# Feed-forward weights that are kept for later, prepared beside the last gates' products instead of beside the branches

## The chip, the cores and the metric

The kernel runs on one core of one Trainium2 chip. The metric is the device time of one execution in microseconds, as the median of several runs. A core has five engines with a queue each: PE (matrix products), DVE (vector), ACT (scalar), POOL (GpSimd) and SP, which here only issues DMA transfers. Every engine takes the instructions of its own queue in order and waits on semaphores for the others.

## The reference

One layer of a decoder trunk on 1040 rows (1024 and 16 meta tokens) of width 1024, in float32. What matters here:

```python
u = rmsnorm(h, mix_norm_pre[l])
proj = u @ w_in[l]
q, f_logit, i_in, g_out, v_pool, gate_a, gate_b = jnp.split(proj, cuts, axis=-1)
a = hgrn2(q, f_logit, i_in, g_out, lbs[l], hgrn_out_norm[l])
p = multiscale_pool(v_pool, pool_proj[l], pool_scale[l])
z = (jax.nn.sigmoid(gate_a) * (a @ w_branch_hgrn[l])
     + jax.nn.sigmoid(gate_b) * (p @ w_branch_pool[l]))
h = h + rmsnorm(z @ w_out[l], mix_norm_post[l])
u = rmsnorm(h, ffn_norm_pre[l])
gt = causal_dwconv(u @ ffn_w_gate[l], ffn_conv_w[l], ffn_conv_b[l])
y = (jax.nn.gelu(gt, approximate=True) * (u @ ffn_w_up[l])) @ ffn_w_down[l]
h = h + rmsnorm(y, ffn_norm_post[l])
```

Every float32 operand of a product is split into two rounded parts (hi and lo, type fp32r), and a product is three matmuls: hi·hi, hi·lo, lo·hi. The split of a weight is a cast on ACT (hi) and a subtraction on DVE (lo).

## The kernel before

The program has these stages in order: norms and the v projection, to about 80 us; the **gates**, to 319.6 us; the **ORDER stage**, to about 552 us; then the product with w_out, the feed-forward part, and the down projection.

*The gates* (class `Strassen`, object `gates`) compute thirteen blocks of `u @ w_in`, named by `GUNITS`: Q0 Q1 G0 A0 A1 A2 F0 F1 A3 B0 B1 B2 B3. Units 8 to 12 are A3, B0, B1, B2, B3. One unit is one level of Strassen's scheme, seven products in the order P1, P2, P6, P5, P3, P7, P4 (24 matmuls of 256 or 258 columns, or 12 of 512), about 19.5 us in all. `product` writes one product into one of four PSUM pairs (`pf`, 4 buffers), then calls `ahead`, which casts and subtracts the weights of the product four places later: names `whi` and `wlo`, three buffers each, two products to a buffer. The raw weights are in `wraw` (three buffers); their Strassen sums `swa`, `swb` are made on GpSimd by `load_unit`, four for a unit. `rest` takes a unit from P6 to P4 and evicts the products on DVE: `p1` += P6; `sg` <- p1, P5 and `sg` += P3 (`put`); `p1` += P7; `sg` <- p1, P5; `sg` <- p1, P4. ACT copies P1 out of PSUM. `between` is a dictionary of functions that `rest` calls after a product; the gates pass none before. In this stage the tile framework's scheduler sets the order of each engine's queue from the program's dependences.

*The ORDER stage* follows a list written by hand: `h0` to `h3` are steps of the four HGRN heads (names `st`, `po`, `al`, `f`, `k`, `q`), `sp` the pooling, PV, G, PP, BB and BA branch products, `sa` the split of a head's output (`ah`, `al`). A `Loader` keeps weight pairs for the products three places ahead: `loader.ahead()` issues the load on SP, the cast on ACT and the subtraction on DVE. Eleven `w` items prepare weights of the feed-forward part: `w0` to `w3` (`keep_first`) split a raw block of the gate matrix; `w4` and `w5` are steps of `keep_unit`, which loads two blocks, makes Strassen sums on DVE and splits them. All results are "kept": `keep` puts them on the list `owed`, and `pay` issues their stores to DRAM (`kept…h`, `kept…l`) on SP. They are read back when the feed-forward products begin. The tiles of the w items are taken from `whi`, `wlo` and `wraw`, and `behind()` places their instructions after the last marked ones of ACT and DVE.

Of the kernel before, what the change touches and what calls it, by code (L numbers as in the profile page):

```python
# [14 lines left out]
P = 128  # L15
# [18 lines left out]
HEADS = 4  # L34
# [13 lines left out]
BEGUN_GATES = 6  # L48
SUMS_AT = {5: (2,), 6: (2, 1), 8: (3,), 9: (1,), 11: (4,), 13: (3,), 14: (1,), 15: (4,), 16: (0,), 17: (0,)}
# [7 lines left out]
ORDER = ("h0 h1 PVp0 PVq0 h0 PVr0 h1 PVs0 h0 PVp1 h1 PVq1 h0 PVr1 h1 PVs1 h0 sp0 PVp2 h1 PVq2 h0 sp1 PVr2 h1 PVs2 "  # L57
# [31 lines left out]
def trunk_kernel(ctx: ExitStack, tc: tile.TileContext, x, meta_tokens, mix_norm_pre,  # L89
# [162 lines left out]
    class Strassen:  # L252
# [96 lines left out]
        lead, whole_pair = 4, False  # L349
# [606 lines left out]
    def keep(*what, lo=None):  # L956

        tiles_ = [wst.tile([P, 1024], F32R, tag="whi", name=nm("whi"))]
        tiles_.append(wst.tile([P, 1024], F32R, tag="wlo", name=nm("wlo")) if lo is None else lo)
        at = [KEPT.index(key) for key, _ in what]  # L960
        with behind():
            for i, (_, src) in enumerate(what):
                hi, lo = (t[:, i * 512 : (i + 1) * 512].rearrange("p (k c) -> p k c", k=4) for t in tiles_)
                if isinstance(src, tuple):
                    for a, op, b in src:
                        dve.tensor_tensor(rr(lo), rr(lo) if a is None else a, rr(lo) if b is None else b, op)
                    src = rr(lo)
                act.copy(hi, src)
                dve.tensor_tensor(lo, src, rr(hi), ALU.subtract)
# [15 lines left out]
    def keep_first(u):  # L985
        raw = wst.tile([P, 1024], F32R, tag="wraw", name=nm("wraw"), bufs=NRAW)
        src = rr(raw).rearrange("p (k c) -> p k c", k=KD)
        nc.sync.dma_start(src, wblock(ffn_w_gate[0], 0, KD, 2 * u * P, P))
        keep(((u, "P1"), src[:, :4]), ((u, "P2"), src[:, 4:]), lo=raw)

    def keep_unit(u, w):
        ab = []
        for h in range(2):
            t = wraw_tile().rearrange("p (k c) -> p k c", k=4)
            nc.sync.dma_start(t, wblock(w, 4 * h, 4, 0, 2 * P))
            ab.append(t)
        a11, a21, a12, a22 = ab[0][:, :, :P], ab[0][:, :, P:], ab[1][:, :, :P], ab[1][:, :, P:]
# [9 lines left out]
        yield  # L1007

    keeps = [keep_unit(0, ffn_w_gate[0]), keep_unit(UP0, ffn_w_up[0])]
# [62 lines left out]
    with tc.manual_schedule(engines={E.Activation, E.DVE, E.PE}):  # L1072
# [178 lines left out]
    with tc.manual_schedule(engines={E.PE}):  # L1251
        for kind, i in order:
# [3 lines left out]
            if kind == "w":  # L1256
                keep_first(i) if i < EARLY else next(keeps[i - EARLY])
                continue
# [42 lines left out]
            pay()  # L1301
# [629 lines left out]
```

## Time and profile before

| | |
|---|---|
| median of 3 runs (lowest to highest) | 1300.82 us (1300.25 to 1304.34) |
| profiled execution: its time, its span | 1301.48 us, 1299.8 us |
| PE busy | 1285.0 us, 99% |
| DVE, ACT, POOL busy | 975.7, 530.2, 371.1 us |
| mean granted PE clock | 0.998 |
| DMA traffic | 248.67 MB, mean 191 GB/s |

In the profile's rows a line gives the start, the duration, the engine, the line of the program, the operation, the tile written and the tiles read, shapes, and in brackets how long the engine sat idle just before and what released it. A window's row gives its length, then the busy time and number of instructions of PE, PE's weight loads, DVE, ACT and POOL, then the clock granted to PE, the busy share of the DMA engines and GB/s. In the list of waits stand engine, line, what was waited for, and total, count and longest in us; "issue" is time in which the engine waited for nothing that the profile shows. Almost all of PE's time is work, so the waits of PE inside a stage say what that stage could give.

### The profile page before, as it was taken

The page shows a single profiled execution, that of the slowest core. Times are in us where ns is not written, and L with a number is a line of the kernel's source. Part 1 is how long each engine was busy: PE and PEld are TensorE (multiplying, and loading weights), DVE is VectorE, ACT ScalarE, POOL GpSimd, SP SyncE. Part 2 cuts the span into 40 slices and gives each one's busy share as a digit, 9 for nine tenths or more (in the row PEclk, how much of TensorE's full clock was granted, in tenths as well). Part 3 has the DMA queues.
Part 4 walks back from the last instruction along what each step waited for, and adds up shares of the span by engine and source line. Part 5 has one row for each costly group of instructions (what it writes and reads, how often), then busy time and mean ns, then how long its engine had stood idle before and what let it go on. Part 6 is the DMA issues. An engine that isn't in the chain of part 4 may idle for free.

```text
span 1299.8 us, 22003 instructions
## 1 busy us (share of the span) xinstructions
PE 1285.0 (99%) x8637; PEld 1133.8 (87%) x8637; DVE 975.7 (75%) x1319; ACT 530.2 (41%) x923; POOL 371.1 (29%) x316
## 2 busy tenths in 40 slices
PE   9999999999999999999999999999999999999998
PEld 7799899999999899978898888888888888888887
DVE  7797569753876877866688999888898885555758
ACT  7553346332245646235563222222232232444443
POOL 3055333320000000250145655454665552000000
PEclk9999999999999999999999999999999999999999
DMA  8144435434523767866877777567777699666644
GB/s 279 42 135 151 146 124 173 164 106 156 154 88 117 241 214 250 318 194 248 283 247 243 207 214 180 155 178 201 184 172 170 148 264 287 209 225 224 229 172 162
DMA packets 145161, 248.67 MB, mean 191 GB/s; under 512 B 11072, under 2 KB 76268, under 8 KB 145058
## 3 DMA queue, kind: packets, MB, share of 16 engines
q1 hardware_dynamic: 127794, 213.42, 48.9%
q0 software_dynamic: 12064, 24.38, 11.2%
q10 hardware_dynamic: 5200, 9.46, 2.0%
q8 instruction: 68, 1.11, 0.3%
q14 instruction: 35, 0.29, 0.1%
HBM read 175.17 MB, written 95.09 MB: 208 GB/s over the span
## 4 chain that ended last, share of the span: by engine, by line
PE 95%; DVE 2%; DMA 1%; ACT 1%; issue 1%; SPq 0%; DVEq 0%; ACTq 0%
PE P L342 18%; PE P L343 18%; PE P L345 18%; PE pd L222 5%; PE pd L224 5%; PE pd L223 5%; PE pm L222 2%; PE pm L224 2%; PE pm L223 2%; PE ppv L242 1%; PE ppv L246 1%; PE ppv L243 1%; PE pv L223 1%; PE pv L222 1%; PE pv L224 1%; PE pba L243 1%
## 5 line engine op out<-in xcount | busy, mean ns | idle before, releaser
L82 ACT CAST whi<-wraw 128x512 fp32r<-128x512 f32 (+2 forms) x141 | 96.5, 707 | 157.8 <-PE P L343 82.7
L343 PE MATMUL P<-v,whi 128*128 128x512 f32 (+2 forms) x408 | 140.7, 353 | 0.0
L342 PE MATMUL P<-v,whi 128*128 128x512 f32 (+2 forms) x408 | 140.7, 352 | 0.0
L345 PE MATMUL P<-v,wlo 128*128 128x512 f32 (+2 forms) x424 | 135.1, 349 | 0.0
L82 DVE TENSOR_TENSOR p<-p,P 128x512 f32<-128x512 f32 (+2 forms) x124 | 84.8, 684 | 41.3 <-PE P L345 40.5
L313 POOL TENSOR_TENSOR swa<-wraw,wraw 128x512 f32<-128x512 f32 x33 | 50.8, 1539 | 193.8 <-DMA wraw<-in_ffn_w_gate_dram 71.3
L82 DVE TENSOR_TENSOR wlo<-wraw,whi 128x512 fp32r<-128x512 f32 (+2 forms) x107 | 93.7, 893 | 8.9 <-ACT whi L82 5.0
L82 DVE TENSOR_TENSOR rot<-wraw,rot 128x1024 fp32r<-128x1024 f32 x31 | 38.0, 1225 | 72.2 <-ACT rot L82 72.2
L342 PEld LDWEIGHTS P<-v,whi 128*128 128x128 f32 x408 | 76.7, 188 | 10.4
L343 PEld LDWEIGHTS P<-v,whi 128*128 128x128 f32 x408 | 76.6, 188 | 10.2
L345 PEld LDWEIGHTS P<-v,wlo 128*128 128x128 f32 x424 | 74.0, 188 | 10.8
L224 PE MATMUL pd<-rot 128*128 128x512 f32 x274 | 82.5, 388 | 0.0
L223 PE MATMUL pd<-rot 128*128 128x512 f32 x274 | 82.5, 387 | 0.0
L222 PE MATMUL pd<-rot 128*128 128x512 f32 x274 | 81.9, 388 | 0.1
L82 DVE TENSOR_TENSOR wlo<-swb,whi 128x512 fp32r<-128x512 f32 x66 | 72.9, 1113 | 4.7 <-ACT whi L82 4.7
L82 ACT CAST whi<-swa 128x512 fp32r<-128x512 f32 x66 | 39.2, 618 | 89.2 <-PE P L343 83.8
L342 PE MATMUL P<-uhi,whi 128*128 128x256 f32 (+3 forms) x260 | 74.6, 304 | 0.0
L343 PE MATMUL P<-ulo,whi 128*128 128x256 f32 (+3 forms) x260 | 74.3, 303 | 0.0
L82 ACT CAST whi<-swb 128x512 fp32r<-128x512 f32 x66 | 39.3, 619 | 77.0 <-PE P L343 67.4
L82 ACT CAST rot<-wraw 128x1024 fp32r<-128x1024 f32 x31 | 32.7, 1054 | 90.8 <-PE pd L224 89.4
L342 PE MATMUL P<-t4h,whi 128*128 128x258 f32 (+2 forms) x236 | 67.6, 303 | 0.0
L343 PE MATMUL P<-t4l,whi 128*128 128x258 f32 (+2 forms) x236 | 67.4, 303 | 0.0
(348 smaller groups left out, 3757.0 us busy)
## 6 DMA issues: line engine op xcount, KB each, us to landing
wraw<-in_w_in_dram SPq DMA_DIRECT2D x38, 512.0 KB, 4.9
yt<-ysum SPq DMA_DIRECT2D x33, 512.0 KB, 4.7
wraw<-in_ffn_w_gate_dram SPq DMA_DIRECT2D x26, 512.0 KB, 7.5
wraw<-in_ffn_w_up_dram SPq DMA_DIRECT2D x22, 512.0 KB, 5.4
wsum<-in_ffn_w_down_dram SPq DMA_DIRECT2D x22, 512.0 KB, 8.7
wraw<-in_w_out_dram SPq DMA_DIRECT2D x18, 512.0 KB, 4.8
ysum<-ys SPq DMA_DIRECT2D x11, 768.0 KB, 7.7
sa<-sscr SPq DMA_DIRECT2D x16, 513.0 KB, 7.7
```

The lines of the kernel that those rows point to most:

```text
L82: self.last = method(*a, **k)
L222: pe.matmul(ps, ahi, bhi, start=first, stop=False)
L223: pe.matmul(ps, ahi, blo, start=False, stop=False)
L224: pe.matmul(ps, alo, bhi, start=False, stop=last)
L242: pe.matmul(ps[:, :n], whi[:, k, :], xhi, start=(k == 0), stop=False)
L243: pe.matmul(ps[:, :n], whi[:, k, :], xlo, start=False, stop=False)
L246: pe.matmul(ps[:, :n], wlo[:, k, :], xhi, start=False, stop=(k == n_k - 1))
L313: pool_e.tensor_tensor(s1, a21, a22, ALU.add)
L342: pe.matmul(d, whi[:, k, :], xh[:, c : c + w], start=(k == 0 and onto is None), stop=False, **go)
L343: pe.matmul(d, whi[:, k, :], xl[:, c : c + w], start=False, stop=False, **go)
L345: pe.matmul(x[:, o : o + w], wlo[:, k, :], xh[:, c : c + w], start=False, stop=(k == 3), **go)
```

## The change

The eleven `w` items leave ORDER. Their steps are made by a new function `keep_step`, which `rest` calls through `beside` after P6, P5, P3 and P7 of units 8, 9 and 10 and after P6 of unit 11; what is left over is done at the end of the gates. Their tiles come from the pool `fm` (26 slots; name `wk`), their sums are made on GpSimd instead of DVE, and `behind()` is left out. Each step first issues the stores that the step before left owed. The first loads now stand one step ahead of their use. In the ORDER stage `pay` goes, and the loader's call after BB7 moves to the last `sa` item, one place later.

```diff
+KEEP_FROM = 8
...
-        lead, whole_pair = 4, False
+        lead, whole_pair, beside = 4, False, {}
...
-                self.rest(u, None, *self.run[i + 2 : i + 3])
+                self.rest(u, self.beside.get(u), *self.run[i + 2 : i + 3])
...
-        tiles_ = [wst.tile([P, 1024], F32R, tag="whi", name=nm("whi"))]
-        tiles_.append(wst.tile([P, 1024], F32R, tag="wlo", name=nm("wlo")) if lo is None else lo)
+        tiles_ = [slot(1024, F32R, "wk"), slot(1024, F32R, "wk") if lo is None else lo]
...
-                        dve.tensor_tensor(rr(lo), rr(lo) if a is None else a, rr(lo) if b is None else b, op)
+                    pool_e.tensor_tensor(rr(lo), rr(lo) if a is None else a, rr(lo) if b is None else b, op)
...
     def keep_first(u):
-        raw = wst.tile([P, 1024], F32R, tag="wraw", name=nm("wraw"), bufs=NRAW)
+        raw = slot(1024, F32R, "wk")
         src = rr(raw).rearrange("p (k c) -> p k c", k=KD)
         nc.sync.dma_start(src, wblock(ffn_w_gate[0], 0, KD, 2 * u * P, P))
+        yield
         keep(((u, "P1"), src[:, :4]), ((u, "P2"), src[:, 4:]), lo=raw)
+        yield "end"
...
-    keeps = [keep_unit(0, ffn_w_gate[0]), keep_unit(UP0, ffn_w_up[0])]
+    keeps = [keep_first(u) for u in range(EARLY)] + [keep_unit(0, ffn_w_gate[0]), keep_unit(UP0, ffn_w_up[0])]
+
+    def keep_step():
+        pay()
+        if keeps and next(keeps[0]) == "end":
+            keeps.pop(0)
+            if keeps:
+                next(keeps[0])
...
+    gates.beside = {u: {p: [keep_step] for p in ("P6", "P5", "P3", "P7")} for u in range(KEEP_FROM, KEEP_FROM + 3)}
+    gates.beside[KEEP_FROM + 3] = dict(P6=[keep_step])
     gates.finish()
+    while keeps or owed:
+        keep_step()
...
+                if i == HEADS - 1:
+                    loader.ahead()
...
-                loader.ahead()
-                pay()
+                if (kind, i) != ("BB", KD - 1):
+                    loader.ahead()
```

How the queues change at the places that matter. First DVE at the end of unit B0 and the beginning of B1, before the change (B0's products are P5_373, P3_376, P7_378 and P4_382, its sums go to p1_366; P2_392 is B1's):

```order
L82 TENSOR_TENSOR sg_377_2820<-p1_366_2698,P5_373_2788 128x512
L82 TENSOR_TENSOR sg_377_2820<-sg_377_2820,P3_376_2805 128x512
L82 TENSOR_TENSOR wlo_380_2839<-swa_363_2688,whi_379_2838 128x512 x2
L82 TENSOR_TENSOR p1_366_2698<-p1_366_2698,P7_378_2825 128x512
L82 TENSOR_TENSOR sg_381_2843<-p1_366_2698,P5_373_2788 128x512
L82 TENSOR_TENSOR sg_387_2884<-p1_366_2698,P4_382_2847 128x514
L82 TENSOR_TENSOR wlo_391_2915<-swb_364_2689,whi_390_2914 128x512 x2
L82 TENSOR_TENSOR sg_393_2946<-p1_388_2888,P2_392_2919 128x514
```

The same place after it (B0's products are P5_383, P3_388, P7_392 and P4_400, B1's P2_410; wk_387 and wk_391 are kept weights, the lo parts of unit 0's P6 and P5, and of its P3 and P7):

```order
L83 TENSOR_TENSOR wlo_409_2994<-swb_371_2720,whi_408_2993 128x512 x2
L83 TENSOR_TENSOR wk_387_2854<-wk_387_2854,wk_386_2853 128x512
L83 TENSOR_TENSOR sg_389_2877<-p1_373_2729,P5_383_2832 128x512
L83 TENSOR_TENSOR wk_387_2854<-wk_387_2854,wk_386_2853 128x512
L83 TENSOR_TENSOR sg_389_2877<-sg_389_2877,P3_388_2862 128x512
L83 TENSOR_TENSOR p1_373_2729<-p1_373_2729,P7_392_2894 128x512
L83 TENSOR_TENSOR wk_391_2885<-wk_391_2885,wk_390_2884 128x512 x2
L83 TENSOR_TENSOR wk_396_2915<-wk_382_2830,wk_395_2914 128x512
L83 TENSOR_TENSOR sg_399_2922<-p1_373_2729,P5_383_2832 128x512
L83 TENSOR_TENSOR sg_405_2963<-p1_373_2729,P4_400_2926 128x514
L83 TENSOR_TENSOR sg_411_3025<-p1_406_2967,P2_410_2998 128x514
```

The subtraction of B1's weights from swb stood behind all reads of B0's products; now it and the kept weights stand ahead of those of P5, P3, P7 and P4.

SP after the change, at the same place (kept…h and kept…l are the stores; wk_381 and wk_382 the raw blocks that the sums in wk_387 and wk_391 read):

```order
L982 DMA kept2h_181<-wk_380_2823 128x512
L982 DMA kept4h_185<-wk_380_2823 128x512
L982 DMA kept2l_182<-wk_363_2680 128x512
L982 DMA kept4l_186<-wk_363_2680 128x512
L996 DMA wk_381_2828<-in_ffn_w_gate_dram 128x4x256
L996 DMA wk_382_2830<-in_ffn_w_gate_dram 128x4x256
L982 DMA kept5h_187<-wk_386_2853 128x1024
```

The loads of unit 0's raw blocks follow the stores of the last `keep_first`; before the change none of these transfers lay in the gates.

In the ORDER stage, DVE about the state update `st` of the last heads, before the change:

```order
L82 TENSOR_TENSOR al_715_5695<-o_558_4468,ah_714_5694 128x1026
L82 SCALAR_TENSOR_TENSOR st_704_5647<-st_704_5647,f_574_4574,ds_706_5651 128x128
L82 TENSOR_TENSOR wlo_696_5582<-wlo_696_5582,wraw_687_5545 128x512
L82 TENSOR_TENSOR wlo_696_5582<-wlo_696_5582,whi_695_5581 128x512
L82 TENSOR_TENSOR sa_691_5558<-sa_691_5558,pbb_711_5673 128x342
L82 TENSOR_TENSOR sa_691_5558<-sa_691_5558,pbb_712_5674 128x342
L82 TENSOR_TENSOR sa_691_5558<-sa_691_5558,pbb_713_5675 128x342
L82 SCALAR_TENSOR_TENSOR st_704_5647<-st_704_5647,f_574_4574,ds_706_5651 128x128
```

and after it (wlo_728 is the split of a BA weight pair):

```order
L83 TENSOR_TENSOR al_725_5744<-o_584_4592,ah_724_5743 128x1026
L83 SCALAR_TENSOR_TENSOR st_716_5700<-st_716_5700,f_600_4698,ds_718_5704 128x128
L83 TENSOR_TENSOR wlo_728_5767<-wraw_726_5765,whi_727_5766 128x1024
L83 SCALAR_TENSOR_TENSOR st_716_5700<-st_716_5700,f_600_4698,ds_718_5704 128x128
L83 TENSOR_TENSOR sa_705_5625<-sa_705_5625,pbb_721_5722 128x342
```

The w item's sums and subtractions (wlo_696) are gone from between the two updates, and the three `sa` products follow the second one.

More of the change, by code (lines that the diff above doesn't have):

```diff
@@ L956, in keep @@
     def keep(*what, lo=None):
-        tiles_ = [wst.tile([P, 1024], F32R, tag="whi", name=nm("whi"))]
-        tiles_.append(wst.tile([P, 1024], F32R, tag="wlo", name=nm("wlo")) if lo is None else lo)
+        tiles_ = [slot(1024, F32R, "wk"), slot(1024, F32R, "wk") if lo is None else lo]
         at = [KEPT.index(key) for key, _ in what]
[L961 to L965, printed above, removed]
-                        dve.tensor_tensor(rr(lo), rr(lo) if a is None else a, rr(lo) if b is None else b, op)
-                    src = rr(lo)
-                act.copy(hi, src)
-                dve.tensor_tensor(lo, src, rr(hi), ALU.subtract)
+        for i, (_, src) in enumerate(what):
+            hi, lo = (t[:, i * 512 : (i + 1) * 512].rearrange("p (k c) -> p k c", k=4) for t in tiles_)
+            if isinstance(src, tuple):
+                for a, op, b in src:
+                    pool_e.tensor_tensor(rr(lo), rr(lo) if a is None else a, rr(lo) if b is None else b, op)
+                src = rr(lo)
+            act.copy(hi, src)
+            dve.tensor_tensor(lo, src, rr(hi), ALU.subtract)
         for h, t in enumerate(tiles_):
@@ L1006, in keep_unit @@
         keep(((u, "P4"), a22))
[L1007 to L1009 removed]
+        yield "end"
+    keeps = [keep_first(u) for u in range(EARLY)] + [keep_unit(0, ffn_w_gate[0]), keep_unit(UP0, ffn_w_up[0])]
[5 more added lines that the diff above has]
+                next(keeps[0])
     order = ORDER.split()
```

9 lines of the change are left out of this document (3 added, 6 removed), and 8 rows, old and new, of the table ORDER.

## The prediction

> **What bounds the kernel now.** I read the busy shares first, then PE's list of waits, then a table of windows, then the timelines of the two stages that the change touches.
>
> ```profile
> PE 1285.0 (99%) x8637; PEld 1133.8 (87%) x8637; DVE 975.7 (75%) x1319; ACT 530.2 (41%) x923; POOL 371.1 (29%) x316
> ...
> PE sl L739 <- issue: 2.4, 1, 2.4
> ...
> PE po L832 <- DVE st L82: 1.5, 1, 1.5
> PE pba L243 <- DVE al L82: 0.6, 1, 0.6
> PE pbb L246 <- issue: 0.6, 1, 0.6
> PE sb L762 <- issue: 0.5, 1, 0.5
> ...
> 227.00:260.00 33.00, 33.00 (x215) 30.19 (x214) 26.14 (x34) 11.63 (x21) 12.34 (x9) 1.00 0.49 161
> 260.00:293.00 33.00, 33.00 (x232) 30.93 (x231) 16.43 (x24) 12.16 (x21) 6.91 (x6) 1.00 0.31 104
> ...
> 489.88:493.29 3.41, 3.41 (x17) 3.41 (x16) 1.74 (x4) 1.71 (x4) 0.00 (x0) 0.50 0.70 273
> ...
> 434.20:436.70 2.50, 0.14 (x16) 0.06 (x9) 0.85 (x3) 2.46 (x4) 0.00 (x0) 1.00 0.99 378
> ```
>
> PE is the bound: it works 1285.0 of 1299.8 us, and the product count does not change. So the change can give back only what PE loses where the work is taken out, and that is small: in the stage of heads and branches the five waits above make 5.6 us, and the window 489.88 to 493.29, granted half the clock, does 1.7 us of work in 3.41. In the last gates' units, where the work is put, PE is busy 33.00 of 33.00 us twice: nothing to gain there, and every wait that appears is a loss. What is idle there are the helpers: in 227 to 260 DVE is busy 26.14, GpSimd 12.34, the DMA 0.49. But it isn't their mean that matters, it is the order of DVE's queue against the PSUM pairs.
>
> **The place that decides: the seam from unit B0 to B1.** PE writes each product into one of four PSUM pairs, so the first product of B1 can start only when the third-product pair of B0 (P3) has been read by DVE's second add into sg. Today:
>
> ```profile
> 250.72 1.29 DVE L82 TENSOR_TENSOR wlo<-wraw,whi 128x512 fp32r<-128x512 f32 x2
> 252.83 0.69 DVE L82 TENSOR_TENSOR sg<-p,P 128x512 f32<-128x512 f32 x1 [0.83 <-PE P L345]
> 255.55 0.69 DVE L82 TENSOR_TENSOR sg<-sg,P 128x512 f32<-128x512 f32 x1 [2.03 <-PE P L345]
> ...
> 261.14 0.69 DVE L82 TENSOR_TENSOR sg<-p,P 128x514 f32<-128x514 f32 x1 [0.78 <-PE P L345]
> 262.13 1.29 DVE L82 TENSOR_TENSOR wlo<-swb,whi 128x512 fp32r<-128x512 f32 x2 [0.30 <-ACT whi L82]
> ...
> 261.48 1.14 ACT L82 CAST whi<-swb 128x512 fp32r<-128x512 f32 x2 [0.45 <-PE P L345]
> ...
> 260.70 0.40 PE L345 MATMUL P<-t4h,wlo 128*128 128x258 f32 x2
> 260.94 0.28 PE L342 MATMUL P<-uhi,whi 128*128 128x258 f32 x1
> ```
>
> P3 is read at 255.55; the pair is wanted at 260.94 when B1 begins; slack 4.7 us. B1's pair of weights from swb is cast at 261.48 and subtracted at 262.13, because its buffer is one of three and is released only by the last product of B0 (the matmuls ending at 260.94). The new order of DVE puts exactly this subtraction (wlo_409) and a subtraction of the kept weights (wk_387) ahead of the two adds of sg_389 that read P5 and P3, with a second wk_387 between them. DVE takes its queue in order. So P3 can't be read before B0 has ended, and B1 can't start before P3 is read: PE must stand still.
>
> **The change, part by part.**
>
> *The floor of that wait, from the order alone.* Casts at 261.48, subtractions over at 262.13 + 1.29 = 263.42, then four DVE instructions at 1.29 / 2 = 0.64 each: 263.42 + 2.6 = 266.0. B1 starts there instead of at 260.94: **5.0 us**, even if every byte is in time.
>
> *The sums on GpSimd and the loads before them.* wk_387 needs three GpSimd sums and two casts; they need two loads of 512 KB, which stand on SP behind the four stores of the pair before, the last of which wait for DVE's wk_363.
>
> ```profile
> L313 POOL TENSOR_TENSOR swa<-wraw,wraw 128x512 f32<-128x512 f32 x33 | 50.8, 1539 | 193.8 <-DMA wraw<-in_ffn_w_gate_dram 71.3
> ...
> DMA to landing us min/median/max: 3.5/5.0/6.6
> ...
> DMA packets 4131, 5.32 MB, mean 161 GB/s; under 512 B 544, under 2 KB 2592, under 8 KB 4128
> ```
>
> The first row is the page's group of today's gate sums (1539 ns each), the second the landing times of the gates' 512 KB loads in 225 to 300 us, the third the traffic of 227 to 260. wk_363 follows the wlo that ends at 252.0 and takes 1.29: 253.3. Two stores and two loads at 0.6 us an issue (two took 1.25 in SP's row of 512.85, below) bring the second load to about 254.4 at the earliest; it lands after 6.6 (I take the largest, since 1 MB of stores goes just ahead): 261.0. Three sums of 1.54: 265.6; a cast of 0.57 (half of the 1.14), a subtraction and the add at 0.69: 267.6. That is 6.7 us of wait in place of 5.0. With the least landing, 3.5, the sums no longer decide and the floor does.
>
> *The DMA traffic.* By 260 the change adds six loads of 512 KB and eight times 512 KB of stores, 7.3 MB, to 5.32 MB: 12.7 MB in 33 us are 384 GB/s, against 378 in the fullest window quoted above (share 0.99). So the transfers stand in line, and the loads are late. No row shows by how much: from 0 to one more landing of 6.6; I take 2, since 12.7 MB at 378 fit into 33.5 us, half a microsecond over, and what makes them late is clustering. The term for B1's first product: **+8.7** (5.0 to 13.3).
>
> *Other gate seams.* The same two kinds of instruction (a wlo whose buffer waits for the running unit, and wk subtractions behind GpSimd sums) stand ahead of B1's sg_399, B2's sg_423 and sg_429. B1's sixth product waits for four more sums (6.2 us) against 5.8 us of P1 and P2 (48 matmuls at 0.12): about 0.5, with the cast and four DVE steps behind it up to 3. B2's first product and P6 have 0 to 2.7 each; but a stall moves PE behind DVE, so that the next one shrinks. **+2.0** (0 to 6). DVE itself gets 20 more subtractions of 0.69, 14 us over the 73 us from 227 to 300, of which it idles well over 20; its share stays below 1 and this costs nothing by itself, as long as no queue order lets PE wait.
>
> *DVE beside GpSimd.* A subtraction with two SBUF inputs is longer while GpSimd sums:
>
> ```profile
> 236.94 0.68 DVE L82 TENSOR_TENSOR wlo<-swa,whi 128x512 fp32r<-128x512 f32 x1
> ...
> 256.16 2.88 DVE L82 TENSOR_TENSOR wlo<-swa,whi 128x512 fp32r<-128x512 f32 x2
> 258.96 0.68 DVE L82 TENSOR_TENSOR p<-p,P 128x512 f32<-128x512 f32 x1
> ...
> 255.49 1.30 POOL L313 TENSOR_TENSOR swa<-wraw,wraw 128x512 f32<-128x512 f32 x1 [8.68 <-DMA wraw<-in_w_in_dram]
> 256.75 1.74 POOL L315 TENSOR_TENSOR swb<-wraw 128x512 f32<-128x512 f32 x1
> 258.45 1.75 POOL L314 TENSOR_TENSOR swa<-swa,wraw 128x512 f32<-128x512 f32 x1
> ```
>
> Two subtractions took 2.88 with GpSimd at work, one alone 0.68, and the add from PSUM beside the 1.75 us sum stayed at 0.68. The two wlo_409 and the two wk_387 lie beside GpSimd's fourth to seventh sum: 0 to 4 x 0.76 = 3 us. Part of it lies behind the wait for the sums; I leave it at 0 in the sum, and in the range.
>
> The Trainium skill's page "SBUF — State Buffer", section "Who interferes with whom", has a rule for this that speaks against the change: a VectorE instruction with two SBUF inputs and a GpSimd instruction that reads SBUF exclude each other for a whole instruction, while one with a PSUM input goes free. The trace agrees (2.88 for two against 0.68). By the rule in full, 3 us more, the forecast below would be 1313.
>
> *Half clock.* After the 1.5 us wait at 487.0 PE ran 3.41 us at 0.50; after the wait of 2.35 at 434.3 it didn't. A stop of nearly 9 us should bring one such window: 3.41 / 2 = **+1.7** (0, or two windows, 3.4).
>
> The Trainium skill's page "TensorE: Matmul & The Clock Gate", section "Part 1: The HAM clock gate", makes it certain rather than likely: after at least one idle window of about 3.4 us the clock is halved, until a busy one has passed. This trace shows the halving after a shorter stop, so its threshold isn't the whole story; the price is the same 1.7.
>
> *What the removal gives back.*
>
> ```profile
> 485.38 0.34 DVE L82 SCALAR_TENSOR_TENSOR st<-st,f,ds 128x128 f32<-128x128 f32 x1
> 485.64 0.68 DVE L82 TENSOR_TENSOR wlo<-wlo,wraw 128x512 f32<-128x512 f32 x1
> 486.24 0.68 DVE L82 TENSOR_TENSOR wlo<-wlo,whi 128x512 fp32r<-128x512 f32 x1
> 486.84 1.35 DVE L82 TENSOR_TENSOR sa<-sa,pbb 128x342 f32<-128x342 f32 x3
> 488.11 0.34 DVE L82 SCALAR_TENSOR_TENSOR st<-st,f,ds 128x128 f32<-128x128 f32 x1
> ...
> 510.40 1.29 DVE L82 TENSOR_TENSOR wlo<-wlo,whi 128x512 fp32r<-128x512 f32 x2
> 511.61 1.22 DVE L82 TENSOR_TENSOR wlo<-wraw,whi 128x1024 fp32r<-128x1024 f32 x1
> ...
> 488.50 0.49 PE L832 MATMUL po<-q,st 128*128 128x128 f32 x2 [1.50 <-DVE st L82]
> ...
> 514.01 0.42 PE L243 MATMUL pba<-al,whi 128*128 128x342 f32 x1 [0.59 <-DVE al L82]
> ...
> 429.89 0.63 PE L246 MATMUL pbb<-uhi,wlo 128*128 128x342 f32 x3 [0.58 <-issue]
> 436.64 0.38 PE L739 MATMUL sl<-q,k 128*32 128x16 f32 x23 [2.35 <-issue]
> ...
> 512.85 1.25 SPq L196 DMA_DIRECT2D wraw<-in_w_branch_hgrn_dram  x2
> ```
>
> The st of 488.11 lies behind two subtractions of a w item and three sa products. In the new order there stand al, st, one wlo of 1.22 (a BA weight pair) and then st: it can be done by 487.1, and PE's 1.50 goes, with the half clock that followed it, 1.7 (and if that window was not its consequence, 0). The 1.29 of w subtractions and the 1.22 of a BA pair leave the queue ahead of al: the 0.59 goes. **−3.8** (−2.1 to −3.8). The two stops put down to "issue" (0.58 and 2.35) have the DMA at 0.99 of its share; the w loads and stores are part of that, but PE waited for nothing that the profile shows. Between 0 and −2.9 I take 0, since no row ties them to w. The 0.5 at sb, in the stage before any w item, stays.
>
> *The BA weight pair a step later.* Loaded at the last "sa", about 510, landed in 6.6, cast and subtracted in 2.3: 519. BA0 starts at 514.01 and two BA products of 36 matmuls of 342 columns, at 0.16 us each (two of 258 columns step by 0.24 between the rows 260.70 and 260.94), take 11.5 us: BA2 is due near 525. Cover 6 us, cost 0; without it the pair would cost what it is late.
>
> **Sum.** The profiled execution took 1301.48 us, 0.66 over the median of 1300.82. 1301.48 + 8.7 + 2.0 + 1.7 − 3.8 = **1310.1**, 0.7% slower. 0.3% (3.9 us) is about what a measurement of this kernel can tell from no change.
>
> **The rivals.**
>
> *Same.* The loads land in 3.5 and only the floor is paid: + 5.0, no half clock, nothing at other seams, − 3.8: 1302.7; with both issue stops gone 1299.8. For it: DMA share 0.49 today. Against it: 384 against 378 GB/s.
>
> *Faster.* P3 is read before the end of B0, because DVE gets wlo_409 early (its buffer free before B0's last product), so that the seam keeps its 4.7 us of slack and only the gains are left: 1301.48 − 3.8 − 2.9 = 1294.8. It decides if sg_389's second add ends ahead of 260.9. Against it: the same cast waits for PE until 261.48 today, and nothing in the change frees that buffer sooner.
>
> *Worse.* The stores ahead of the loads clog the queues: B1 waits 13.3, the other seams 6, two half-clock windows 3.4, less 3.8: 1320.4. For it: the 384 GB/s, and loads that stand on one queue behind stores that wait for DVE.
>
> *The edit does nothing.* The work hides in both places, and PE neither waits nor gains: 1301. The order speaks against it, as with "faster".
>
> **Chances.** Forecast 0.58; worse 0.24; same 0.10 and nothing 0.02; faster 0.06. Cases above 1304.7 hold the first two: slower 0.82, same 0.12, faster 0.06. The range has to leave out "faster" and what is above "worse" with its 3 us of DVE: from the same-case's 1302 to 1323.
>
> **What would show it.** Right: PE's list of waits headed by P on a DVE sg add, 5 to 13 us long at about 261, followed by a window with clock 0.50; the DMA share in 227 to 260 near 0.9 or above; po's and pba's waits gone; windows of the gates no longer 33.00. Wrong: sg_389 read before 261, or PE idle at the seam under 4 us, or loads issued before 252. If the two issue stops vanish too, my zero for them was wrong by 2.9; if they stay, they never belonged to w.

## The result: 1.8% slower, lost in the gates

Five runs of the changed kernel had a median of 1326.33 us (1322.62 to 1329.72), against 1302.56 for the kernel before beside it (1300.25 to 1304.34). The ratio is 1.0184, 95% interval 1.0173 to 1.0195. The forecast of 1310.1 had the sign, the place and the mechanism, but 0.7% in place of 1.8%; the time lies 3 us above the range. The profiled execution took 1326.33 us, with a span of 1324.6.

The page's row of busy times after the change:

```profile
PE 1291.8 (98%) x8637; PEld 1140.3 (86%) x8637; DVE 975.4 (74%) x1305; ACT 530.4 (40%) x923; POOL 386.1 (29%) x330
```

PE runs the same 8637 matmuls and is busy 6.8 us longer: some of them ran at a lower clock. To see in which stage the time went, take the first matmul into two tiles: ppv is the first product of the ORDER stage, pm the first after it. The rows give count, durations, then first and last start. Before:

```profile
L242 PE MATMUL ppv<-uhi,whi x96: 317/322/430, 319.6 to 378.3; 128*128 128x346 f32 x64, 128*128 128x348 f32 x32
...
L222 PE MATMUL pm<-whi,zc x128: 389/389/500, 552.6 to 651.8; 128*128 128x512 f32 x128
```

After:

```profile
L243 PE MATMUL ppv<-uhi,whi x96: 317/322/430, 348.9 to 407.4; 128*128 128x346 f32 x64, 128*128 128x348 f32 x32
...
L223 PE MATMUL pm<-whi,zc x128: 389/389/500, 577.4 to 676.7; 128*128 128x512 f32 x128
```

The gates end at 348.9 instead of 319.6, +29.3 us. ORDER takes 577.4 − 348.9 = 228.5 instead of 233.0, −4.5. What follows takes 747.2 in both. So nearly the whole loss is in the stage that received the work, and the removal did give something back.

PE's list of waits after the change (total, times, longest, in us):

```profile
PE P L343 <- DVE sg L83: 17.3, 3, 13.4
PE P L343 <- ACT p L83: 4.6, 1, 4.6
...
PE sl L740 <- issue: 1.3, 1, 1.3
```

The four P waits, 21.9 us, all lie in the gates and are new. Two stand at the first product of a unit (276.50 in B1, 301.19 in B2), two at its third, P6 (249.00 in B0, 313.14 in B2). Before, PE waited nowhere in these units. The matmuls that ended them:

```profile
249.00 0.36 PE L343 MATMUL P<-t2h,whi 128*128 128x258 f32 x1 [0.89 <-DVE sg L83]
...
276.50 0.55 PE L343 MATMUL P<-uhi,whi 128*128 128x258 f32 x1 [13.39 <-DVE sg L83]
...
301.19 0.55 PE L343 MATMUL P<-uhi,whi 128*128 128x258 f32 x1 [3.06 <-DVE sg L83]
...
313.14 0.55 PE L343 MATMUL P<-t2h,whi 128*128 128x258 f32 x1 [4.56 <-ACT p L83]
```

A table of windows shows the rest (length; busy PE, PEld, DVE, ACT, POOL; then the granted clock, the DMA share and GB/s):

```profile
227.00:260.00 33.00, 32.12 (x206) 29.17 (x205) 26.66 (x40) 16.87 (x31) 6.64 (x5) 1.00 0.97 304
240.00:260.00 20.00, 19.11 (x129) 17.57 (x128) 13.76 (x20) 9.90 (x19) 5.87 (x4) 1.00 1.09 338
276.40:280.70 4.30, 4.20 (x20) 4.23 (x21) 1.82 (x3) 2.00 (x4) 3.88 (x4) 0.52 0.47 183
301.19:304.60 3.41, 3.41 (x16) 3.41 (x17) 3.41 (x3) 1.13 (x2) 3.33 (x4) 0.52 0.42 157
313.14:318.30 5.16, 5.16 (x25) 5.16 (x26) 1.06 (x2) 1.78 (x4) 0.00 (x0) 0.52 0.81 304
464.60:468.00 3.40, 3.40 (x33) 3.37 (x34) 1.63 (x4) 2.21 (x5) 0.00 (x0) 0.54 1.07 274
```

The first row is the stretch ahead of the long wait: the DMA's share went from 0.49 to 0.97; the second row is its last 20 us (the profile's shares can pass 1). The next three are the windows of half clock behind the last three waits: 4.20 + 3.41 + 5.16 = 12.8 us of PE time at a granted 0.52, so about 6.1 lost. 21.9 + 6.1 = 28.0 of the 29.3. Another 0.7 lies ahead of the gates, whose first matmul starts at 65.1 instead of 64.3; the rest is not attributed. The last row lies in ORDER, behind the 1.3 us stop at sl.

Now the seam from B0 to B1 itself. SP's queue (the loads that the sums read are the last row; kept…h and kept…l are the stores):

```profile
251.33 0.34 SPq L982 DMA_DIRECT2D kept3h<-wk  x1
...
260.92 0.32 SPq L982 DMA_DIRECT2D kept4h<-wk  x1
...
262.78 1.06 SPq L996 DMA_DIRECT2D wk<-in_ffn_w_gate_dram  x2
```

and what SP waited for between 245 and 265:

```profile
SPq L982 <- ACT wk L83: 3.3, 2, 1.9
SPq L982 <- DMA kept3h<-wk: 3.2, 1, 3.2
```

The loads were issued at 262.78 and 263.2, where the prediction had 254.4 for the second. Part of it is a late weight: ACT, DVE, GpSimd and again DVE in the timeline,

```profile
250.16 1.15 ACT L83 CAST wk<-wk 128x512 fp32r<-128x512 f32 x2 [3.37 <-DMA wk<-in_ffn_w_gate_dram]
...
250.81 2.75 DVE L83 TENSOR_TENSOR wk<-wk,wk 128x512 fp32r<-128x512 f32 x2 [1.35 <-ACT wk L83]
...
256.59 1.29 DVE L83 TENSOR_TENSOR wk<-wk,wk 128x512 fp32r<-128x512 f32 x2
...
263.62 1.29 DVE L83 TENSOR_TENSOR wlo<-swb,whi 128x512 fp32r<-128x512 f32 x2 [4.28 <-ACT whi L83]
...
269.84 5.37 POOL L965 TENSOR_TENSOR wk<-wk,wk 128x512 f32<-128x512 f32 x4 [15.12 <-DMA wk<-in_ffn_w_gate_dram]
...
273.00 1.09 DVE L83 TENSOR_TENSOR wk<-wk,wk 128x512 fp32r<-128x512 f32 x1 [8.09 <-ACT wk L83]
274.01 0.67 DVE L83 TENSOR_TENSOR sg<-p,P 128x512 f32<-128x512 f32 x1
274.61 1.15 DVE L83 TENSOR_TENSOR wk<-wk,wk 128x512 fp32r<-128x512 f32 x1
275.68 0.68 DVE L83 TENSOR_TENSOR sg<-sg,P 128x512 f32<-128x512 f32 x1
```

ACT waited 3.37 us for a kept weight's load that landed late, DVE's two subtractions behind it took 2.75 beside GpSimd, and the subtraction of the last keep_first pair, wk_363, ended at 256.59 + 1.29 = 257.9 in place of 253.3. The other part is SP itself: it waited for late casts, and 3.2 us, up to the row of 260.92, for the store issued at 251.33, which was still open. From the landing on everything went as the queue order said: sums from 269.84, subtraction 273.00, the read of P3 over at 275.68 + 0.68 = 276.36, and B1's first product at 276.50. DVE's instruction ahead of them all, the subtraction from swb, had been done since 264.9. So the order that the prediction read is the order that ran, but what PE waited for in the end was the loads.

### The profile page after: what moved, and what is told of

Same layout as the page of the kernel before. It is cut to its first block, busy times and chain, and to the rows that moved or that the text cites. A ratio compares the mean times of both kernels' runs of the same rounds, so it can differ in the third digit from the quotient of the medians.

```text
span 1324.6 us, 22030 instructions
## 1 busy us (share of the span) xinstructions
PE 1291.8 (98%) x8637; PEld 1140.3 (86%) x8637; DVE 975.4 (74%) x1305; ACT 530.4 (40%) x923; POOL 386.1 (29%) x330
## 4 chain that ended last, share of the span: by engine, by line
PE 90%; DVE 4%; DMA 2%; issue 2%; ACT 1%; POOL 1%; DVEq 0%; SPq 0%; POOLq 0%; ACTq 0%
PE P L343 16%; PE P L344 15%; PE P L346 15%; PE pd L223 5%; PE pd L225 5%; PE pd L224 5%; PE pm L223 2%; PE pm L225 2%; PE pm L224 2%; PE ppv L243 1%; PE pbb L243 1%; PE pbb L244 1%; PE pba L243 1%; PE pbb L247 1%; PE pba L244 1%
## 5 line engine op out<-in xcount | busy, mean ns | idle before, releaser
L83 ACT CAST whi<-wraw 128x512 fp32r<-128x512 f32 (+2 forms) x129 | 89.5, 715 | 150.4 <-PE P L344 76.1
L343 PE MATMUL P<-t2h,whi 128*128 128x258 f32 (+2 forms) x236 | 68.6, 308 | 5.4 <-ACT p L83 4.6
L344 PE MATMUL P<-t2l,whi 128*128 128x258 f32 (+2 forms) x236 | 68.2, 306 | 0.0
```

Source lines behind the costliest of these rows:

```text
L83: self.last = method(*a, **k)
L343: pe.matmul(d, whi[:, k, :], xh[:, c : c + w], start=(k == 0 and onto is None), stop=False, **go)
L344: pe.matmul(d, whi[:, k, :], xl[:, c : c + w], start=False, stop=False, **go)
```

## The experiments

All are edits of the changed kernel except e8. "ppv" is when the gates ended. e1, e2, e3 and e5 store constants in place of the kept weights, or of most of them.

| run | edit in words | median us | ratio to before (95%) | ppv |
|---|---|---|---|---|
| e1 | no kept work in the gates | 1296.57 | 0.9961 (0.9949 to 0.9973) | 320.1 |
| e2 | no stores in the gates | 1306.33 | 1.0036 (1.0023 to 1.0049) | 328.6 |
| e3 | stores from a constant tile | 1308.08 | 1.0046 (1.0031 to 1.0061) | 330.7 |
| e4 | sums on DVE | 1321.12 | 1.0149 (1.0118 to 1.0180) | 340.3 |
| e5 | stores of 1/16 the size | 1313.79 | 1.0089 (1.0061 to 1.0117) | 333.4 |
| e6 | one step at the end of each unit | 1308.91 | 1.0041 (1.0025 to 1.0057) | 331.8 |
| e7 | steps at the ends of units 8 to 11 | 1324.05 | 1.0173 (1.0154 to 1.0192) | 344.8 |
| e8 | before, with the loader edit alone | 1300.32 | 0.9987 (0.9976 to 0.9998) | 319.9 |
| e9 | ends of units 0 to 5 and 8 to 12 | 1303.49 | 1.0013 (1.0004 to 1.0023) | 325.8 |
| e10 | two steps a unit in 0 to 5 | 1317.10 | 1.0117 (1.0102 to 1.0133) | 339.3 |
| e11 | as e9, behind P6 | 1301.58 | 0.9998 (0.9990 to 1.0007) | 324.1 |
| e12 | as e11, none in units 6 to 8 | 1297.45 | 0.9960 (0.9946 to 0.9975) | 319.4 |
| e13 | the kept stores on ACT's queue | 1324.06 | 1.0173 (1.0152 to 1.0195) | 346.2 |

**What the removal is worth, and what the place costs (e1, e2, e3).**

```diff
 e1
-    gates.beside = {u: {p: [keep_step] for p in ("P6", "P5", "P3", "P7")} for u in range(KEEP_FROM, KEEP_FROM + 3)}
-    gates.beside[KEEP_FROM + 3] = dict(P6=[keep_step])
-    while keeps or owed:
-        keep_step()
+                later()        # in ORDER: two 512 KB stores from a constant tile
```

> The kept weights are not prepared at all: no loads, sums, casts or subtractions in the gates or in the ORDER stage; the 20 stores of 512 KB are made in the ORDER stage from one tile of constants, so that their bytes stay. It shows what taking the w items out gives. Theory (the gate stage pays all of the loss, the ORDER stage gains what the changed kernel shows there, 4.5 us): gates as before with PE never idle, about 1297 us, 1295 to 1299. Rival (the ORDER stage's stops have other causes and the 4.5 us are partly chance): 1300 to 1302.

Measured 1296.57, with no kept weight to wait for, one wait of 0.5 us in the gates, and the gates over at 320.1. So the removal, with the loader's edit, is worth 0.4%, and the change as made pays about 30 us for its place.

```diff
 e2
-        while owed:
-            nc.sync.dma_start(*owed.pop(0))
+        owed.clear()
...
+                later()        # as in e1
```

> The changed kernel, with loads, sums, casts and subtractions beside the gates, but its stores there are left out and made in the ORDER stage from a tile of constants; the scheduler then also puts DVE's read of P3 ahead of the late subtraction from swb. Theory (transfers decide: loads of the kept blocks stand behind the stores): unit 0's two loads go out near 254 us instead of 263, B1's wait falls from 13.4 to under 4 us, the three other gate waits to under 3 in all, at most one half-clock window: 1298 to 1307. Rival (GpSimd's sums and the subtractions in DVE's queue decide): the wait stays over 8 us, 1312 to 1325.

Without the stores beside the gates the wait at the seam is 2.04 us; the loads were issued at 251.09 in place of 262.78:

```profile
251.09 1.02 SPq L1002 DMA_DIRECT2D wk<-in_ffn_w_gate_dram  x2
...
264.48 0.36 PE L343 MATMUL P<-uhi,whi 128*128 128x258 f32 x1 [2.04 <-DVE sg L83]
```

The stores, or what stands for them in the queues, carry most of the loss. But one thing besides differs: in this kernel the scheduler also set DVE's read of P3 ahead of the subtraction from swb. So e2 does not measure the 5.0 us floor.

```diff
 e3
-            nc.sync.dma_start(*owed.pop(0))
+            to, t = owed.pop(0)
+            nc.sync.dma_start(to, rr(dummy)[:, : t.shape[1]])
```

> The changed kernel with every store beside the gates at its old place in the program and of its old size, but from a tile of constants, so that no store waits for DVE or ACT; DVE's order about the seam is that of the kernel without stores. Theory A (the bytes on the DMA queues make the loads late): gates lose 15 to 27 us, 1312 to 1324. Theory B (the stores hold up SP because they wait for DVE's subtractions, the bytes don't matter): as without stores, 1298 to 1307. Theory C (DVE's order is the cause, its floor of 5 us and what follows): 1300 to 1315, with loads landing as late as in the changed kernel.

This was to keep the bytes and take away only the stores' wait for DVE. The scheduler moved the stores out of the place: 12.44 MB were moved in 225 to 300 us, about the 12.76 of the kernel without stores. It is a second e2 (longest wait 4.17), and does not answer its question.

**Sums on GpSimd or on DVE (e4).**

```diff
 e4
-                    pool_e.tensor_tensor(rr(lo), rr(lo) if a is None else a, rr(lo) if b is None else b, op)
+                    dve.tensor_tensor(rr(lo), rr(lo) if a is None else a, rr(lo) if b is None else b, op)
```

> The changed kernel with the 14 sums on DVE again, all else as it is. Theory (the loads land at 269.8 and the order of DVE's queue does the rest): each sum takes 0.6 to 0.7 us on DVE instead of 1.3 to 1.7, so that B1's wait falls by 1 to 3 us from 13.4, the other waits by as much: 1320 to 1326. Rival (GpSimd's slow sums, and the time that DVE loses beside them, make the loss): 1303 to 1316.

```profile
274.20 0.55 PE L343 MATMUL P<-uhi,whi 128*128 128x258 f32 x1 [11.60 <-DVE sg L83]
```

The long wait stays, 11.60 instead of 13.39: GpSimd is not its cause. The two later ones fell from 3.06 and 4.56 to 1.27 and 1.90. Why GpSimd cost something there is in the changed kernel's timeline of the next seam:

```profile
301.54 2.96 POOL L965 TENSOR_TENSOR wk<-wk,wk 128x512 f32<-128x512 f32 x2
...
301.56 1.80 DVE L83 TENSOR_TENSOR wlo<-swa,whi 128x512 fp32r<-128x512 f32 x1
303.28 1.77 DVE L83 TENSOR_TENSOR wlo<-swb,whi 128x512 fp32r<-128x512 f32 x1
...
312.49 0.59 ACT L83 COPY p<-P 128x514 f32<-128x514 f32 x1 [4.76 <-DVE wk L83]
```

Each DVE subtraction takes 1.75 to 1.80 us beside GpSimd's sums, against 0.68 alone, and five such stand in a row there (301.56 to 310.1), ahead of ACT's copy of P1, for which PE waited 4.56 and which the trace has released by a kept subtraction on DVE. The copy reads no kept weight; its target p1 is a tile of the pool fm, as the kept tiles are, so a wait for a slot fits.

**The bytes or the queue order (e5).**

```diff
 e5
-            nc.sync.dma_start(*owed.pop(0))
+            to, t = owed.pop(0)
+            n = t.shape[1] // 16
+            nc.sync.dma_start(to[:, :n], t[:, :n])
```

> The changed kernel with every store beside the gates cut to a sixteenth of its columns (it still waits for the same DVE or ACT instruction, on the same queue); the full blocks are stored once from a tile of constants, which the scheduler puts early in the gates. Theory A (the bytes in 230 to 262 us keep the earlier transfers open, and SP waits for those): unit 0's loads go out by 255 us, B1's wait is under 4 us, 1303 to 1309. Theory B (SP is held up because the stores wait for DVE's subtractions, whatever their size): the loads go out after 259 us, B1 waits over 7 us, 1313 to 1325.

```profile
253.00 1.71 SPq L998 DMA_DIRECT2D wk<-in_ffn_w_gate_dram  x2
...
261.77 5.37 POOL L965 TENSOR_TENSOR wk<-wk,wk 128x512 f32<-128x512 f32 x4 [10.42 <-DMA kept4l<-wk]
...
268.44 0.55 PE L343 MATMUL P<-uhi,whi 128*128 128x258 f32 x1 [6.87 <-DVE sg L83]
...
270.54 2.36 DVE L83 TENSOR_TENSOR wlo<-swb,whi 128x512 fp32r<-128x512 f32 x2
```

With small stores the loads are issued at 253.0 and 254.3, where the prediction put them, 9.8 and 8.9 us earlier than with full ones, and the wait is 6.87. That this is near the 6.7 of the prediction's chain of load, sums, cast and reads is chance. The sums did start at 261.77, close to the 261.0 assumed, but the profile has them released by a small store, kept4l, issued at 256.88, and not by the loads; and DVE's subtraction from swb stands behind the read of P3 (267.62) here, as it does without stores. The scheduler also moved the loads ahead of the last four stores, so part of the earlier issue is order. Neither expectation came whole: the loads went out as in A, the wait lies near B's 7 and the time in B's range.

**The same work elsewhere (e6, e7).**

```diff
 e6
+            then("end")        # in rest, behind the unit's last evicted product
...
-    gates.beside = {u: {p: [keep_step] for p in ("P6", "P5", "P3", "P7")} for u in range(KEEP_FROM, KEEP_FROM + 3)}
-    gates.beside[KEEP_FROM + 3] = dict(P6=[keep_step])
+    gates.beside = {u: dict(end=[keep_step]) for u in range(len(GUNITS))}
```

> The changed kernel with the 13 steps at the ends of the 13 units, one each, instead of four to a unit in units 8 to 11. Same instructions, same bytes, GpSimd sums too. Theory (too much in too short a stretch, and ahead of evictions): the DMA share stays under 0.8 in every 20 us of the gates, PE loses under 2 us in the gates, and the ORDER stage gives its 4.5: 1297 to 1300. Rival (each step in DVE's queue costs PE a wait wherever it stands, above all in the units F0 and F1 where DVE is busy all the time): 1306 to 1325.

1308.91, in the rival's range. No wait in units 0 to 5, and none over 0.3 us in B0 to B3; the others stand in F1 and A3 (units 7 and 8), the longest of them:

```profile
218.28 0.62 ACT L83 CAST wk<-wk 128x512 fp32r<-128x512 f32 x1 [1.43 <-POOL wk L966]
218.81 0.59 ACT L83 COPY p<-P 128x528 f32<-128x528 f32 x1
...
219.45 0.79 PE L343 MATMUL P<-uhi,whi 128*128 128x512 f32 x1 [4.44 <-ACT p L83]
```

ACT's cast waits for GpSimd, and the copy of P1 out of PSUM stands behind it, so PE waits 4.44: the mechanism of the prediction, on another queue. The DMA's share from 200 to 220 was 0.53, so this wait is not one of a full DMA.

```diff
 e7
-    gates.beside = {u: {p: [keep_step] for p in ("P6", "P5", "P3", "P7")} for u in range(KEEP_FROM, KEEP_FROM + 3)}
-    gates.beside[KEEP_FROM + 3] = dict(P6=[keep_step])
+    gates.beside = {u: dict(end=[keep_step] * (4 if u < KEEP_FROM + 3 else 1)) for u in range(KEEP_FROM, KEEP_FROM + 4)}
```

> The changed kernel with the same steps in the same units, but each unit's four steps behind its last eviction instead of behind P6, P5, P3 and P7. Theory (the order in DVE's queue is the first cause, the bytes the second): the 13.4 us at B1's first product go, waits of B1's and B2's second and sixth products behind late kept weights stay, 6 to 16 us in all: 1304 to 1316. Rival (bytes alone): loads as late as before, the wait only moves: 1320 to 1328.

Steps behind all reads of a unit's products take DVE's sg out of the story, and the time stays, as the rival had it: 4.86, 7.22 and 5.87 us, all on ACT's copy of P1. The copies stand behind casts of kept weights, and the second, at 287.53, waited its last 1.33 us, by the profile, for the store of kept5l, though it reads only PSUM; its target p1 is a tile of the pool fm. The queue changes, the price does not, as long as four steps are crowded into one unit.

**The edit of the loader (e8).**

```diff
 e8, the kernel before with
+                if i == HEADS - 1:
+                    loader.ahead()
...
-                loader.ahead()
+                if (kind, i) != ("BB", KD - 1):
+                    loader.ahead()
```

> The kernel before with one edit of the change alone: the loader's call after BB7 moves to the last sa item. Theory (cover of 6 us, cost 0): 1300 to 1303.5, no wait of a BA product on its weights. Rival (the pair comes late, or the SP queue is full there): 1304 to 1307; other rival (part of the 4.5 us that the ORDER stage gives comes from this edit): 1297 to 1299.5.

0.9987 (0.9976 to 0.9998), and no BA product waits for its weights: the later pair costs nothing. It may give something back: the interval stands for 0.3 to 3.1 us, and the wait of 0.59 at pba is gone with this edit alone, since al (at 510.26) now goes ahead of the BA split (at 511.40).

**Towards a better place (e9 to e12).**

```diff
 e9, e10, e12: with then("end") as in e6; the old lines of gates.beside go in all four
 e9
+    gates.beside = {u: dict(end=[keep_step] * n) for u, n in {0: 1, 1: 1, 2: 1, 3: 1, 4: 1, 5: 1, 8: 2, 9: 1, 10: 1, 11: 2, 12: 1}.items()}
 e10
+    gates.beside = {u: dict(P6=[keep_step], end=[keep_step] * (1 + (u == 5))) for u in range(6)}
 e11: as e9, with P6 in place of end, and {8: 1, 9: 2, 10: 1, 11: 2, 12: 1}
 e12
+    gates.beside = {u: dict(P6=[keep_step]) for u in range(6)}
+    gates.beside[0]["end"] = [keep_step]
+    gates.beside.update({u: dict(P6=[keep_step] * n) for u, n in {9: 2, 10: 1, 11: 2, 12: 1}.items()})
```

> The changed kernel with one step at the end of each of units 0 to 5, none in the two F units (where DVE and ACT are full and the spread kernel lost its time), then two, one, one, two and one at the ends of units 8 to 12. Theory (the loss is a matter of room: no wait where the loads land before DVE or ACT come to them): gates within 2 us of the kernel before, 1296 to 1300, faster than before. Rival (ACT's copy of the next P1 waits behind casts of kept weights in units 8 to 12 as in the kernel with the steps at the units' ends): 1303 to 1312.

Gate waits of 0.29, 1.99 and 0.61, 1303.49: nearly all of the loss is gone. In the profiled execution the gates still end 6.2 us later than before, with a window of 0.67 of the clock behind the wait of 1.99, and in ORDER the stop of 2.0 at sl brought another (0.67), which e1 did not have after a stop of the same length.

> The changed kernel with all steps in units 0 to 5, two to a unit (behind P6 and at the end), one more at the end of unit 5. Theory (room): these units have GpSimd's and DVE's time to spare, the bytes make about 290 GB/s; waits of PE under 3 us in all: 1297 to 1302. Rival (two steps in 14 us of products are as dense as the change itself, four in 19.5): loads late, waits at the seams of units 1 to 5, 1305 to 1322.

1317.10: two steps a unit are too many in the first units as well, with waits of 0.90, 8.73 and 5.70, as the rival had it. So it is the crowding and not the last units as such.

> As the kernel with six steps, then five units, but each step behind P6 instead of at the unit's end. Theory (the place inside a unit matters by what stands behind it: here the evictions of P3 and P7 do, not the copy of the next P1): like that kernel where the loads are early, with 0 to 3 us more in units 8 to 12, where sums come late: 1297 to 1303. Rival (behind P6 is always worse, since P3's read then waits for the kept weights): 1305 to 1315.

1301.58, waits of 0.42 in A3 (unit 8) and 1.90 at the seam from A3 to B0.

> As the kernel with each step behind P6, but the step of unit A3 (where PE lost 1.9 and 0.4 us and one half-clock window, since the leftovers of F0 and F1 still fill DVE) goes ahead of the F units: unit 0 has two steps, units 1 to 5 one, F0, F1 and A3 none, B0 to B3 two, one, two and one. Theory (room, and nothing else): the gates lose under 1 us and the ORDER stage gives its 4 to 5: 1296.5 to 1299.5, about 0.3% faster than before. Rival (a step taken forward makes a wait in units 4 and 5, where the heavier sums now stand): 1301 to 1306.

1297.45, 0.9960 (0.9946 to 0.9975): faster than both kernels, and as fast as leaving the work out (1296.57). PE's longest wait behind the gates, the two stage rows, and the fullest 20 us of the gates:

```profile
PE sl L741 <- issue: 0.8, 1, 0.8
```

```profile
L243 PE MATMUL ppv<-uhi,whi x96: 317/322/430, 319.4 to 378.2; 128*128 128x346 f32 x64, 128*128 128x348 f32 x32
...
L223 PE MATMUL pm<-whi,zc x128: 389/389/500, 546.3 to 645.5; 128*128 128x512 f32 x128
```

```profile
120.00:140.00 20.00, 20.00 (x123) 17.93 (x122) 14.32 (x22) 7.71 (x14) 6.82 (x5) 1.00 1.00 323
```

The kept weights, their sums and their stores are those of the changed kernel; only where they stand differs. PE is busy all of the window, though the DMA's share is 1.00 at 323 GB/s, little under the 1.09 and 338 of the changed kernel from 240 to 260. The transfers of kept tiles that were issued from 118 to 142 landed in 6.2 to 7.5 us, and ACT waited 4.4 us there for such a load. So a full DMA and late landings do not by themselves cost PE anything. What differs is how long before its use a load goes out: in units 0 to 5 most steps are a unit's five products apart, about 14 us, while in the changed kernel a step follows the one before it by one product (P5 starts at 251.92, P3 at 254.65: 2.7 us), less than a transfer takes. This fits e7 and e10 as well, but B0 and B2 take two steps at once here and lose nothing either, and the distance was not varied by itself.

**SP's queue or the transfers (e13).** What was still open: do the loads come late because they stand on SP behind stores that wait, or because the transfers themselves are late?

```diff
 e13
-            nc.sync.dma_start(*owed.pop(0))
+            act.dma_start(*owed.pop(0))
```

> The changed kernel with the kept stores issued from ACT's queue instead of SP's: same bytes, same sources, and DVE's order at the seam from B0 to B1 word for word that of the changed kernel, with the subtraction from swb ahead of the reads of P5 and P3. Theory S (the stores hold up SP, by their place in its queue and by earlier transfers that are still open): unit 0's loads go out by 253 us and B1's wait falls from 13.4 to 5 to 8 us, not under the 5.0 that the order alone asks for: 1307 to 1317. Theory T (the bytes make the loads themselves slow, whatever queue they are on): they land 9 us or more after they are issued, the wait stays over 9 us, 1318 to 1327.

1324.06, 1.0173 (1.0152 to 1.0195). The loads that the sums read have no kept store ahead of them on SP, and are as late as in the changed kernel:

```profile
260.82 3.20 SPq L996 DMA_DIRECT2D wk<-in_ffn_w_gate_dram  x2
...
278.07 0.55 PE L343 MATMUL P<-uhi,whi 128*128 128x258 f32 x1 [8.17 <-DVE sg L83]
```

SP now waits for other things, between 245 and 265 above all for DVE, for a load of w_in and, with a load of a kept block, for an earlier store; the loss is spread over two places, P6 of B0 and the first product of B1 (5.86 + 8.17 against 0.89 + 13.39):

```profile
SPq L307 <- DVE wlo L83: 8.1, 2, 5.9
SPq L307 <- DMA wraw<-in_w_in_dram: 3.9, 1, 3.9
SPq L987 <- DMA kept1l<-wk: 3.0, 1, 3.0
```

Neither theory came whole: the loads were not out by 253, and the time lies in T's range, but the loads landed in 8.7 us at most and the wait at B1 is 8.17. The stores' place in SP's queue is not the cause of the loss: with it gone, the time is nearly the same. The stores still hold up a load, which takes a new tile of the pool fm: that is a wait for a slot, and not for a place in the queue. What fits the runs is that steps crowded into one stretch wait for each other's transfers and sums, on whichever queue they stand, and that PE loses where a read that frees a PSUM pair stands behind them.

## Why the prediction was right in kind and wrong in size

**What bounds the kernel, the place, the mechanism: right.** PE stood still at the seam from B0 to B1 because DVE's read of P3 stood behind kept subtractions in an in-order queue. The list of waits, the clock and the DMA share show what the last part of the prediction asked for, and the longest wait is a little over its 13 us.

**The first step that failed: "two stores and two loads at 0.6 us an issue bring the second load to about 254.4 at the earliest", with +2 for the DMA traffic.** It came at 263.2. The step counted SP's own issues, and took wk_363 at the time that before's queue gave. Both ends moved: the subtraction ended 4.6 us later (257.9 for 253.3), because an earlier kept load landed late, and SP lost most of the remaining 4 us in its wait of 3.2 for an open store. The prediction had the crowding on the page, 384 GB/s asked against 378 in the fullest window of before, and priced it as half a microsecond over; the rows show one late transfer holding up the next step and its stores. The term was 8.7 and measured 13.4, just above its upper bound of 13.3. The rest of the chain held: from the issue 6.6 us to the start of the sums (269.84 − 263.2), the 6.6 that was taken, and then 6.5 to the end of P3's read, where 6.6 was worked out; e5 has the same 6.5 from the start of its sums (261.77 to 268.30). This term alone would have left the time within the range. What carried it out are the next two terms: 14.6 us together, where 3.7 were forecast and 9.4 was the bound.

**The second, other seams, +2.0: 8.5** (0.89 + 3.06 + 4.56), above the bound of 6. Two reasons show. First, the sum set DVE beside GpSimd at zero; with the sums on DVE two of these waits lost 1.8 and 2.7 us (e4). The Trainium skill, "SBUF — State Buffer", section "Who interferes with whom", says that a VectorE instruction with two SBUF inputs and GpSimd reads exclude each other; the trace agrees (1.75 to 1.80 against 0.68), and leaving it at zero was a mistake of the sum. Second, a wait on ACT's copy of P1 was not looked for; e6 and e7 show how much hangs on that copy. That "a stall moves PE behind DVE, so that the next one shrinks" did not hold.

**The third, half clock, +1.7: about 6.1** in the gates, since all three longer waits were followed by it, and one more window of 1.6 in ORDER. The rule weighed in the prediction, of "TensorE: Matmul & The Clock Gate", section "Part 1: The HAM clock gate" in the Trainium skill, asks for at least one idle window of about 3.4 us. The 13.4 and 4.6 us waits agree with it; halving after 3.06, and after the 1.3 at sl, does not.

**The removal, −3.8: −4.5, and −6.1 where no half clock follows.** The second state update now follows the BA split and no longer the sa products, in the order that was read from the queue:

```profile
511.95 0.34 DVE L83 SCALAR_TENSOR_TENSOR st<-st,f,ds 128x128 f32<-128x128 f32 x1
512.21 1.22 DVE L83 TENSOR_TENSOR wlo<-wraw,whi 128x1024 fp32r<-128x1024 f32 x1
513.34 0.34 DVE L83 SCALAR_TENSOR_TENSOR st<-st,f,ds 128x128 f32<-128x128 f32 x1
```

and the waits at po and pba are gone (pba's by the loader's edit alone, e8). The zero for the stops put down to issue was partly wrong: pbb's 0.58 is gone and sl's 2.35 is 1.3. In e12 it is 0.8, and its ORDER takes 546.3 − 319.4 = 226.9, 6.1 less than before: 1.50 + 0.59 + 0.58 + 1.54 + 1.7 of half clock make 5.9 of it. The changed kernel gives 1.6 of it back in the window behind sl.

**The BA pair a step later, cost 0: right** (e8).

**The rivals.** "Worse" was the nearest, 1320.4 with a chance of 0.24: it named the stores that clog the queues, and had 13.3 for the long wait, but 6 and 3.4 where 8.5 and 6.1 came. "Same", "faster" and "does nothing" fell with the first wait. The floor of 5.0 us from the order alone never showed by itself: in the runs that kept that order (e4, e13) the loads were later still, and e2, e3 and e5 changed the order. It stays open.

**What also stays open.** How much of the delay is the landing of transfers, SP's wait for open ones, the short way from a load to its use, or the slots that hold the kept tiles is not separated. The slots were not in the prediction, and several rows point at them: by the profile DVE waited 5.42 us at 293.8 for the store of kept7l before it wrote another kept tile, SP 3.0 us for kept1l in e13, and ACT's copy in e7 for kept5l. A pool with more slots was not tried.

## What to carry to other kernels

Before work is moved beside a bound engine, add up the bytes that each short stretch will carry: close to the best rate seen, reckon with late transfers, and ask how long before its use each load goes out and who waits for it. Place small steps far enough apart that a load issued one step ahead has landed, and not where the engines' mean idle time is largest: the same instructions and bytes cost 29 us in four units and nothing over ten, even with the DMA full for 20 us. And in an in-order queue ask which instruction that frees a PSUM pair stands behind the moved one, on DVE and on ACT alike.

## What the hardware showed that was not expected

The clock is not decided by the length of a stop alone: PE ran at about half after stops of 1.3 us (after the change, sl) and 1.5 (before, po), and not after 1.98 (e1, sl) or 2.35 (before, sl). The stop at sl in e1 and what follows it:

```profile
436.60:440.00 3.40, 3.40 (x51) 3.16 (x54) 1.92 (x5) 1.69 (x5) 0.00 (x0) 1.00 0.91 227
```

against e9, where the same stop was 2.0 us:

```profile
442.30:445.60 3.30, 3.30 (x37) 3.27 (x38) 1.62 (x4) 1.83 (x5) 0.00 (x0) 0.67 0.95 247
```

What decides besides the length stays open.

The transfers of kept tiles, loads and stores together, landed in 5.3 to 9.2 us (median 6.5) in 245 to 300 of the changed kernel; in e2, where only the loads are left there, in 4.5 to 4.8. In e12 they took 6.2 to 7.5 in the fullest stretch, and PE lost nothing by it. And a queue that only issues transfers stood 3.2 us for one of its own earlier ones: issuing isn't free of the transfers' time.
